# Order of the input norm's squares, one weight load and a small cast behind the splits of x, in a hybrid decoder block

## The chip, the cores and the metric

One core of a Trainium2 chip runs the whole block. The metric is the device time of one launch in microseconds (us): 1686.27 us, the median of 3 runs of the kernel before (1686.22 to 1686.97).

## The reference, cut to what matters

The block takes x (1024 tokens by 1024 channels, float32), forms u = rms_norm(x) and multiplies it with a wide weight matrix w_in, whose columns feed attention, a gated convolution and merge gates:

```python
def rms_norm(x, g):
    y = x * rsqrt(mean(x * x, axis=-1) + EPS)
    return y * g

u = rms_norm(h, norm_mix_g)
z = u @ w_in
q, kc, vc, ks, vs, kw, vw, nsa_g, glu_in, merge_g = split(z, offsets)
y_a = nsa_attention(...) @ w_a
y_b = conformer_conv(glu_in, ...) @ w_b
h = h + (sigmoid(g_a) * y_a + sigmoid(g_b) * y_b) @ w_o
```

After that come a convolutional feed-forward part, a gated per-layer input and a last norm. The change lies in the first 40 us, at the first rms_norm and the first two products of z.

## The kernel before, in words

**Layout.** Channels lie on the 128 partitions and tokens in the free dimension. x is loaded transposed, as KD = 8 tiles of 128 channels by 1024 tokens (tile names H for the first four, M for the last four).

**Split numbers.** A float32 product is made from two reduced-precision parts. `split_gain` (L190) makes from a tile of x, times the norm's gain, a high part uh on ScalarE (L193) and a low part ul on VectorE (L194); all of them carry the tile names U. `load_w` (L123) loads 128 columns of a weight matrix with a DMA of the SP queue (L125), and `split_w` makes wh on ScalarE (L119) and wl on GpSimd (L120). `product` (L133) then issues for each of the 8 tiles of x six matmuls of 512 tokens: wh with uh (L139) and wh with ul (L140) for each half of the tokens, and wl with uh for both halves (L142). So a product has 48 matmuls.

**The norm's factor comes late.** The splits use x and the gain alone. The factor Rs = 1/sqrt(mean x^2 + EPS) is multiplied in when a product leaves PSUM. For it, `add_sq` (L207) squares each half of a tile on ScalarE (L198 for the first tile, L201 for the others) and adds it to one of two running sums, sq[0] on VectorE and sq[1] on GpSimd (both L202). The temporary squares have the tag PW, of which there are four buffers, two of them held by the sums. `rstd_part` (L163) then does for each half of the tokens: eight small matmul instructions with ones (L170), a VectorE step (L172), a power on GpSimd (L173), eight small matmul instructions that spread the factor over the partitions (L176), and a copy into Rs on ScalarE (L178).

**Order at the start.** L212 to L234 load the first weights, then the eight tiles of x with their splits (the first two tiles half by half); after the sixth tile the second weights are loaded. The squares of tile k are queued behind the split of tile k + 2 with `queued_after` (L183), which fixes the order on an engine's queue and waits for nothing. The order on all engine queues is fixed when the program is built, by a list scheduler that follows a modelled timeline and prefers earlier lines among the instructions that are ready; every engine then works its own queue strictly in that order.

**What follows.** A loop over j (L360 to L375) makes two products for each of four column groups of the gated convolution; below they are called pa0, pb0, pa1, pb1, pa2 and so on. They share two PSUM buffers (psA). For j = 0 ScalarE copies the product out of PSUM at once (L355) and VectorE multiplies it by Rs later (L356); for the others VectorE multiplies by Rs straight out of PSUM (L358), so such a product's buffer is free only after Rs is known. VectorE's next long work, the 31-tap convolution (L330, L333), is queued behind that. The positions are loaded by two small DMAs (L262, L263), cast to float on VectorE (L266) and turned into sines and cosines (L270 to L288).

Of the kernel before, what the change touches and what calls it, by code (L numbers as in the profile page):

```python
# [17 lines left out]
P = 128  # L18
T = 1024
D = 1024  # L20
KD = D // P
# [11 lines left out]
C_Q, C_KC, C_VC, C_SEL, C_WIN, C_GLU, C_GA, C_GB = 0, 512, 640, 768, 1024, 1304, 2328, 3352  # L33
# [22 lines left out]
def block_kernel(ctx, tc, xT, pT, pos, par_d, w_in, ck1, ck2, cv1, cv2, w_a, w_b, w_o, w_up, w_down,  # L56
                 w_pg, w_pp, outT):
    nc = tc.nc
# [21 lines left out]
    def t(tag, shape, dt=F32):  # L80
        count[0] += 1
        return where.get(tag, sb).tile(shape, dt, name=f"{tag}_{count[0]}", tag=tag, bufs=BUFS.get(tag, 1))
# [33 lines left out]
    def split_w(raw, shape, hi_tag="wh", lo_tag="wl", eng=nc.gpsimd):  # L116
        hi = t(hi_tag, shape, F32R)
        lo = t(lo_tag, shape, F32R)
        nc.scalar.activation(hi, raw, AF.Copy)  # L119
        eng.tensor_tensor(lo, raw, f(hi), op=OP.subtract)  # L120
        return hi, lo

    def load_w(src, shape, hi_tag="wh", lo_tag="wl", raw_tag="raw", eng=nc.gpsimd):  # L123
        raw = t(raw_tag, shape)
        nc.sync.dma_start(raw, src)  # L125
        return split_w(raw, shape, hi_tag, lo_tag, eng)
# [17 lines left out]
    def wcols(w, c0, n, k0=0, k1=KD):  # L144
        return w[k0 * P:k1 * P, c0:c0 + n].rearrange("(k p) c -> p k c", p=P)
# [37 lines left out]
    def queued_after(*marks):  # L183

        st = ExitStack()
        for m in marks:
            st.enter_context(tc.issue_after(m.ins))
        return st

    def split_gain(j, src, goff, uh, ul):  # L190

        g = par[:, goff + j:goff + j + 1]
        hi = nc.scalar.activation(uh, src, AF.Copy, scale=g)  # L193
        return hi, nc.vector.scalar_tensor_tensor(ul, src, g, f(uh), op0=OP.mult, op1=OP.subtract)  # L194
# [12 lines left out]
    def add_sq(j, src, sq, *engs):  # L207
        for hf in range(2):
            add_sq_half(j, src, sq, hf, engs[hf % len(engs)])
# [7 lines left out]
    xts, split_marks = [], []  # L217
    w_first = load_w(wcols(w_in, C_GLU, P), [P, KD, P])
    for k in range(KD):
        xt = t("H" if k < 4 else "M", [P, T])  # L220
        for s in HALF if k < 2 else [slice(0, T)]:
            nc.sync.dma_start(xt[:, s], xT[k * P:(k + 1) * P, s])
            marks = split_gain(k, xt[:, s], O_GMIX, uh[k][:, s], ul[k][:, s])
        xts.append(xt)
        split_marks.append(marks)
        if k == 5:
            w_second = load_w(wcols(w_in, C_GLU + 512, P), [P, KD, P])
    for k in range(KD):
        with queued_after(*split_marks[min(k + 2, KD - 1)]):
            add_sq(k, xts[k], sq, nc.vector, nc.gpsimd)  # L230
    norm_marks = [m for m in rstd(sq) if m.ins.engine != nc.vector.engine]
    nc.vector.tensor_scalar(rTs, rT, 0.125, None, op0=OP.mult)
# [27 lines left out]
    posi = sb.tile([P, NP], I32, name="posi")  # L260
# [2 lines left out]
    nc.sync.dma_start(posi[0:N_CMP, NCH:NP],  # L263
                      bass.AP(tensor=pos.tensor, offset=pos.offset + 31, ap=[[16, N_CMP], [1, 1]]))
    posf = sb.tile([P, NP], F32, name="posf")
    nc.vector.tensor_copy(posf, posi)  # L266
    tg = t("PW", [P, 256])
    inv = tg[:, 0:8]
    for i in range(8):
# [642 lines left out]
    with tc.manual_schedule(engines={nc.tensor.engine, nc.scalar.engine, nc.vector.engine, nc.gpsimd.engine}):  # L912
# [8 lines left out]
        for i in range(-1, len(jobs)):  # L921
# [6 lines left out]
            for s in range(n):  # L928
                rest = None
                k = s - (n - len(outs))  # L930
# [666 lines left out]
```

## Time and profile before

| what | value |
|---|---|
| median of 3 runs | 1686.27 us |
| the profiled execution's own time | 1692.59 us |
| its span in the profile | 1690.9 us |
| TensorE busy in it | 1636.3 us, 97% |
| VectorE, ScalarE, GpSimd busy | 1189.1, 712.7, 668.7 us |
| mean granted TensorE clock | 0.989 of full speed |

The span is what the hardware profiler saw of one execution; the execution itself took 1.7 us more, and it is 6.3 us above the median of the runs without a profile. PE is TensorE, DVE VectorE, ACT ScalarE, POOL GpSimd and SP the engine that issues the DMAs. A busy engine is one with an instruction in progress, so a PE that is busy at half its clock still counts as busy: the granted clock has to be read beside it.

### The profile page before, as it was taken

To read this page: it belongs to the slowest core of one execution; us is meant where nothing else is said; L and a number is where in the kernel's file an instruction comes from. 1 tells how busy PE (TensorE), PEld (TensorE's weight loads), DVE (VectorE), ACT (ScalarE), POOL (GpSimd) and SP (SyncE) were. 2 spreads that over 40 slices of the span, in tenths; PEclk is the share of its full clock that TensorE was granted. 3 is DMA by queue.
4 is the path that set the end of the run, shared out by engine and by line. 5 is a ranking of instruction groups with operands and counts; after the bars stand their busy time and mean duration, and the time that the engine had idled before them with its cause. 6 is when DMAs were issued, how large, how long until landed. Compare 5 with 4: busy or idle time off the path is not lost.

```text
span 1690.9 us, 23161 instructions
## 1 busy us (share of the span) xinstructions
PE 1636.3 (97%) x8506; PEld 1377.1 (81%) x8506; DVE 1189.1 (70%) x1885; ACT 712.7 (42%) x1202; POOL 668.7 (40%) x602
## 2 busy tenths in 40 slices
PE   7999989999999999999999999999999999999997
PEld 5888989888888788877877888888888778888887
DVE  6799895355677777653368766766667878887756
ACT  6222343555566655523345333343334322223522
POOL 5524345344443343346441232222322344445600
PEclk9999999999999999999999999999999999999998
DMA  6122212322111221146443333333333844443113
GB/s 204 51 63 65 76 54 63 116 82 61 45 52 54 72 76 51 45 162 199 132 154 115 112 100 121 116 100 112 100 115 127 319 149 143 142 141 117 45 38 125
DMA packets 172378, 178.03 MB, mean 105 GB/s; under 512 B 24936, under 2 KB 138728, under 8 KB 172264
## 3 DMA queue, kind: packets, MB, share of 16 engines
q1 hardware_dynamic: 171400, 173.40, 32.0%
q10 hardware_dynamic: 864, 3.15, 0.5%
q8 instruction: 67, 1.10, 0.3%
q14 instruction: 47, 0.39, 0.1%
HBM read 128.29 MB, written 48.23 MB: 104 GB/s over the span
## 4 chain that ended last, share of the span: by engine, by line
PE 82%; DVE 5%; issue 4%; POOL 3%; ACT 3%; DMA 3%; SPq 0%; POOLq 0%; DVEq 0%; ACTq 0%
PE psB L1123 8%; PE psB L1125 8%; PE psB L1124 8%; PE psF L694 7%; PE psO L1428 4%; PE psO L1427 4%; PE psO L1430 4%; PE psA L142 4%; PE psA L140 4%; PE psA L139 4%; PE psO L888 3%; PE psS L791 3%; PE psPT L877 3%; PE psF L728 3%; PE psA L131 3%
## 5 line engine op out<-in xcount | busy, mean ns | idle before, releaser
L1011 POOL TENSOR_TENSOR A<-r,A 128x512 fp32r<-128x512 f32 x65 | 114.4, 1760 | 315.2 <-ACT A L1007 315.2
L120 POOL TENSOR_TENSOR wl<-raw,wh 128x1024 fp32r<-128x1024 f32 (+1 forms) x58 | 143.9, 2483 | 142.3 <-ACT wh L119 142.2
L333 DVE SCALAR_TENSOR_TENSOR conv<-PS,par,conv 128x1023 f32<-128x1023 f32 (+14 forms) x120 | 152.6, 1272 | 3.5
L882 DVE TENSOR_TENSOR PT<-psPT,PT 128x512 fp32r<-128x512 f32 (+1 forms) x136 | 91.6, 674 | 76.6 <-ACT PT L879 75.4
L1007 ACT ACTIVATE S<-psX 128x512 fp32r<-128x512 f32 x88 | 52.6, 598 | 211.7 <-DVE psX L1056 139.0
L119 ACT ACTIVATE wh<-raw 128x1024 fp32r<-128x1024 f32 (+1 forms) x58 | 61.3, 1058 | 148.3 <-PE psA L140 66.5
L694 PE MATMUL psF<-U,wh 128*128 128x512 f32 x352 | 118.9, 400 | 0.0
L879 ACT ACTIVATE PT<-psPT 128x512 fp32r<-128x512 f32 (+1 forms) x136 | 79.3, 584 | 91.3 <-PE psPT L877 86.0
L1161 DVE SCALAR_TENSOR_TENSOR M<-H,par,M 128x1023 f32<-128x1023 f32 x88 | 115.0, 1308 | 0.1
L1123 PE MATMUL psB<-T,S 128*128 128x512 f32 x264 | 104.3, 395 | 5.0 <-DVE H L1166 5.0
L791 PE MATMUL psS<-K,Q 128*128 128x384 f32 (+3 forms) x384 | 105.7, 356 | 0.0
L1125 PE MATMUL psB<-T,S 128*128 128x512 f32 x264 | 104.2, 395 | 0.0
L1124 PE MATMUL psB<-T,S 128*128 128x512 f32 x264 | 103.5, 392 | 0.0
L1428 PE MATMUL psO<-fs,X 128*128 128x512 f32 x256 | 100.5, 392 | 2.4 <-DVE fs L1264 2.4
L1427 PE MATMUL psO<-fs,X 128*128 128x512 f32 x256 | 100.4, 392 | 0.0
L139 PE MATMUL psA<-U,wh 128*128 128x512 f32 x224 | 90.1, 403 | 8.2 <-ACT U L193 7.9
L1011 DVE TENSOR_TENSOR S<-psX,S 128x512 fp32r<-128x512 f32 x88 | 60.7, 690 | 50.3 <-ACT S L1007 50.3
L888 PE MATMUL psO<-PT,V 128*128 128x256 f32 x528 | 91.7, 291 | 2.7 <-DVE PT L882 2.6
L812 POOL TENSOR_SCALAR PS<-PS,rr,gates 128x128 f32<-128x128 f32 (+7 forms) x64 | 52.2, 825 | 103.0 <-DVE rr L808 59.9
L140 PE MATMUL psA<-U,wh 128*128 128x512 f32 x224 | 89.8, 402 | 3.0 <-DVE U L194 3.0
L1166 DVE TENSOR_TENSOR H<-PW,psB 128x512 f32<-128x512 f32 x66 | 45.3, 687 | 55.2 <-PE psB L1125 55.0
L1260 POOL TENSOR_TENSOR F<-F,F 128x1024 f32<-128x1024 f32 x18 | 43.3, 2405 | 100.7 <-issue 74.3
(464 smaller groups left out, 4905.6 us busy)
## 6 DMA issues: line engine op xcount, KB each, us to landing
r<-in_w_up SPq DMA_DIRECT2D x44, 512.0 KB, 4.8
raw<-in_w_in SPq DMA_DIRECT2D x32, 512.0 KB, 3.6
g_d<-M SPq DMA_DIRECT2D x22, 512.0 KB, 2.6
a_d<-M SPq DMA_DIRECT2D x22, 512.0 KB, 3.0
raw<-in_w_o SPq DMA_DIRECT2D x16, 512.0 KB, 4.0
F<-g_d SPq DMA_DIRECT2D x16, 512.0 KB, 4.2
F<-a_d SPq DMA_DIRECT2D x16, 512.0 KB, 3.4
raw<-in_w_down SPq DMA_DIRECT2D x16, 512.0 KB, 4.2
```

The source lines that it names most:

```text
L120: eng.tensor_tensor(lo, raw, f(hi), op=OP.subtract)
L139: nc.tensor.matmul(pz[:, s], hi, xh[k][:, s], start=k == 0, stop=False)
L140: nc.tensor.matmul(pz[:, s], hi, xl[k][:, s], start=False, stop=False)
L333: nc.vector.scalar_tensor_tensor(a[:, s:], y[:, :T - s], w, a[:, s:], op0=OP.mult, op1=OP.add)
L694: nc.tensor.matmul(pz, wa[:, k, :], ua[k][:, s], start=k == 0 and i == 0, stop=k == KD - 1 and i == 2)
L791: nc.tensor.matmul(pS[:, :n * P], Q[:, h, v, :], K[:, i0 * P:(i0 + n) * P], start=v == 0, stop=v == 1)
L1011: return eng.tensor_tensor(o[:, 1, :], src, f(o[:, 0, :]), op=OP.subtract)
L1123: nc.tensor.matmul(pz, hi, xh, start=first and k == 0, stop=False, skip_group_check=True)
L1124: nc.tensor.matmul(pz, hi, xl, start=False, stop=False, skip_group_check=True)
L1125: nc.tensor.matmul(pz, lo, xh, start=False, stop=last and k == 3, skip_group_check=True)
L1427: nc.tensor.matmul(pd, ws[i][0][:, js], fs[i][0][:, s], start=i == 0, stop=False)
L1428: nc.tensor.matmul(pd, ws[i][0][:, js], fs[i][1][:, s], start=False, stop=False)
```

## The change

All eight splits of x come first on ScalarE and VectorE. The second weights' load is moved from behind the sixth tile of x to behind the eighth, and what it puts on ScalarE is queued behind the last split there. All the norm's squares and VectorE's part of their sums are queued behind the last split, instead of behind the split two tiles on. The positions' cast on VectorE is queued behind the last split too.

```diff
             marks = split_gain(k, xt[:, s], O_GMIX, uh[k][:, s], ul[k][:, s])
         xts.append(xt)
         split_marks.append(marks)
-        if k == 5:
-            w_second = load_w(wcols(w_in, C_GLU + 512, P), [P, KD, P])
+    x_split = split_marks[-1]
+    with queued_after(*x_split):
+        w_second = load_w(wcols(w_in, C_GLU + 512, P), [P, KD, P])
     for k in range(KD):
-        with queued_after(*split_marks[min(k + 2, KD - 1)]):
+        with queued_after(*x_split):
             add_sq(k, xts[k], sq, nc.vector, nc.gpsimd)
...
     posf = sb.tile([P, NP], F32, name="posf")
-    nc.vector.tensor_copy(posf, posi)
+    with queued_after(*x_split):
+        nc.vector.tensor_copy(posf, posi)
```

`x_split` holds the last ScalarE and the last VectorE instruction of the splits, so GpSimd's and SP's queues get no such edge: GpSimd's share follows through the data that it needs, and the DMAs follow the order of the lines.

## Rows read from the trace of the kernel before

**Rows 1.** The profile's first part: busy us, share of the span, instructions, by engine.

```profile
PE 1636.3 (97%) x8506; PEld 1377.1 (81%) x8506; DVE 1189.1 (70%) x1885; ACT 712.7 (42%) x1202; POOL 668.7 (40%) x602
```

**Rows 2.** Waits, 0 to 60 us: total us, times, longest.

```profile
PE psA L140 <- DVE U L194: 3.0, 3, 1.8
```

**Rows 3.** Stretches: length, busy by engine (instructions), granted clock, DMA share, GB/s.

```profile
24.33:29.01 4.68, 4.68 (x14) 3.71 (x14) 3.98 (x4) 1.86 (x4) 2.76 (x2) 0.64 0.52 132
...
30.00:100.00 70.00, 70.00 (x320) 57.35 (x319) 53.20 (x57) 21.16 (x25) 36.06 (x20) 1.00 0.23 64
```

**Rows 4.** Timeline of TensorE: start, length (us), operation, [idle before <- releaser].

```profile
14.58 0.40 PE L139 MATMUL psA<-U,wh 128*128 128x512 f32 x1
...
24.33 0.50 PE L140 MATMUL psA<-U,wh 128*128 128x512 f32 x1 [1.83 <-DVE U L194]
...
38.34 0.95 PE L170 MATMUL psF<-ones,PW 128*128 128x1 f32 x8
...
39.70 0.40 PE L139 MATMUL psA<-U,wh 128*128 128x512 f32 x1
...
43.83 0.72 PE L170 MATMUL psF<-ones,PW 128*128 128x1 f32 x6
...
51.44 1.05 PE L176 MATMUL psPT<-ident,rT 128*128 128x128 f32 x8
...
53.50 0.39 PE L139 MATMUL psA<-U,wh 128*128 128x512 f32 x1
...
64.71 0.40 PE L139 MATMUL psA<-U,wh 128*128 128x512 f32 x1
```

**Rows 5.** Timeline of VectorE, 18 to 62 us: splits, the cast, a sum, an evacuation.

```profile
18.40 1.28 DVE L194 SCALAR_TENSOR_TENSOR U<-M,par,U 128x1024 fp32r<-128x1024 f32 x1
19.60 1.26 DVE L266 CAST posf<-posi 128x9 f32<-128x9 int32 x1
20.91 3.37 DVE L194 SCALAR_TENSOR_TENSOR U<-M,par,U 128x1024 fp32r<-128x1024 f32 x1
...
32.19 1.34 DVE L202 TENSOR_TENSOR PW<-PW,PW 128x512 f32<-128x512 f32 x1 [0.70 <-ACT PW L201]
...
61.20 1.23 DVE L358 TENSOR_TENSOR Q<-psA,Rs 128x1024 f32<-128x1024 f32 x1
```

**Rows 6.** Timeline of GpSimd, 18 to 39 us: sums and a low part of weights.

```profile
18.97 1.86 POOL L202 TENSOR_TENSOR PW<-PW,PW 128x512 f32<-128x512 f32 x1 [2.86 <-ACT PW L201]
20.79 2.40 POOL L120 TENSOR_TENSOR wl<-raw,wh 128x1024 fp32r<-128x1024 f32 x1
...
36.91 1.28 POOL L202 TENSOR_TENSOR PW<-PW,PW 128x512 f32<-128x512 f32 x1
```

**Rows 7.** Timeline of ScalarE, 21 to 54 us.

```profile
21.83 1.13 ACT L193 ACTIVATE U<-M,par 128x1024 fp32r<-128x1024 f32 x1
...
28.93 1.18 ACT L201 ACTIVATE PW<-M 128x512 f32<-128x512 f32 x2 [0.51 <-POOL PW L202]
30.97 1.18 ACT L201 ACTIVATE PW<-M 128x512 f32<-128x512 f32 x2 [0.85 <-POOL PW L202]
33.41 1.06 ACT L119 ACTIVATE wh<-raw 128x1024 fp32r<-128x1024 f32 x1 [1.25 <-PE psA L140]
...
39.81 0.26 ACT L288 ACTIVATE cosT<-PW 128x72 f32<-128x72 f32 x1 [1.00 <-DVE PW L287]
...
52.53 0.60 ACT L178 ACTIVATE Rs<-psPT 128x512 f32<-128x512 f32 x1 [6.34 <-PE psPT L176]
```

**Rows 8.** Timeline of SP's queue: DMA issues of the second weights and the last two x tiles.

```profile
7.07 0.38 SPq L125 DMA_DIRECT2D raw<-in_w_in  x1
7.78 3.41 SPq L222 DMA_DIRECT2D M<-in_xT  x2
```

**Rows 9.** DMA issues (6.9 to 7.4, 7.4 to 10.7 us): count, size, us to landing.

```profile
raw<-in_w_in SPq DMA_DIRECT2D x1, 512.0 KB, 9.0
...
M<-in_xT SPq DMA_DIRECT2D x1, 512.0 KB, 9.6
```

## The prediction

> **What bounds the kernel now.** I read the shares of busy time first: TensorE is busy for 97% of the span and no other engine for more than 70% [rows 1], so time can be won mainly where TensorE waits or runs at half clock. The table by stretches comes next: from 30 to 100 us TensorE is busy without a gap at full clock [rows 3]. Whatever it is ahead by at 35 us it can therefore keep, as long as nothing else is late in that stretch. Last I read the timelines of the four engines up to 65 us, which hold the changed lines. The reader should see a collision there. TensorE has its longest wait of the start, 1.83 us, until 24.33 us, for the low split of the seventh tile of x [rows 2, 4]. That split took 3.37 us on VectorE where the one before took 1.28 us, and in front of it the nine-element cast of the positions took 1.26 us [rows 5]. Beside the cast GpSimd was adding squares until 20.83 us, and the cast ends at 20.86 us; beside the slow split GpSimd was making the second weights' low part until 23.19 us, and the split ends 1.09 us later [rows 5, 6]. After that wait TensorE ran for 4.68 us at a mean granted clock of 0.64, so partly at the lower of its two levels, 1.2 and 2.4 GHz; before the drop it had been waiting [rows 3, 4].
>
> By the Trainium skill, page "SBUF — State Buffer", section "Who interferes with whom", a VectorE instruction with two SBUF inputs and a GpSimd instruction that reads SBUF exclude each other for a whole instruction. The two pairs of rows just named agree with it. If the slow split had another cause that stays, the eighth low part would come 2.1 us later than reckoned below, 0.3 us after TensorE wants it, and the sum would be 0.3 us smaller.
>
> **What the splits gain.** Products pa0 and pb0 have 96 matmuls. I count 12 issued before the one at 14.58 us, so 84 lie between it and the first of pa1 at 39.70 us: 25.12 us [rows 4]. At full clock a product of 48 takes 64.71 - 53.50 = 11.21 us, or 0.2335 us a matmul [rows 4]. 84 of them are 19.62 us; with 0.95 us for the eight small matmuls of the norm that stand among them [rows 4] it is 20.57 us. **So 4.55 us are there to be won.** About 1.7 us of it is the half clock (4.68 x 0.36), 2.3 us are waits, the rest is the restart after each.
>
> Is the data there in time? DMA: the second weights were issued at 7.07 us and landed 9.0 us later, at 16.1; the seventh tile was issued at 7.78 and landed at 17.4 [rows 8, 9]. All are 512 KB, so in the new order the seventh tile takes the place at 16.1 us, the eighth that at 17.4, the weights follow 1.3 us later at 18.7. SP's queue issues as many DMAs as before, and the positions' two stay behind them. Splits: with nothing in between, the eighth tile's high part is done at 17.4 + 1.13 = 18.5 us [rows 7] and the low part at 19.8 (1.28 us, no GpSimd beside it [rows 5]). TensorE, from 14.58 us on without a gap, comes to the eighth tile after 30 matmuls, at 21.6 us. Cover 1.8 us: cost nothing, and if a landing slips by more than that, every further microsecond shows. Second weights: the high part takes 1.06 us [rows 7], from 18.7 us or behind the first tile's two squares, so 19.8 to 20.9; the low part takes 2.40 us [rows 6], so 22.2 to 23.3. TensorE wants the high part at 23.0 and the low part four matmuls later, at 23.9. I take nothing; the ends are 0 and 1 us. The cast runs for a moment behind the last split; the sines that use it are not wanted by these products: nothing, either end below 0.3 us.
>
> **What the squares cost.** Sixteen squares, seven VectorE sums and seven GpSimd sums move behind 18.5 us. With four PW buffers the pace is the alternation that the rows show near the end: 2.04 us from one pair of squares to the next (28.93 to 30.97) [rows 7]. The first GpSimd sum waits for the second weights' low part, so it ends at 23.5 to 24.6 us; six more pairs take 12.2 us: 35.7 to 36.8 us, and 2.40 us more if pa1's low part is put between them as now, so 38.1 to 39.2. Before it was 36.91 + 1.28 = 38.2 us [rows 6]. VectorE's sum, last done at 33.5 us before [rows 5], comes about 1 us ahead of GpSimd's, so 34.7 to 38.2 us. TensorE's first small matmuls (L170) stood at 38.34, those of the second half at 43.83 [rows 4]; 4.55 us earlier that is 33.8 and 39.3. If the first keep their place in TensorE's queue, they wait 0.9 to 4.4 us, and every product matmul waits behind them; if the scheduler moves them back with the squares, nothing. TensorE never waited for them before, and stood 4.8 us behind the sum. The same modelled order sees the squares later, so I take 0.5 us, near the lower end; the ends are 0 and 4.4.
>
> **What is late next.** Rs's second half was made at 52.53 us, behind small matmuls that stood at 51.44 us in TensorE's order [rows 4, 7]. VectorE then empties pa1 until 61.20 + 1.23 = 62.43 us [rows 5], and pa2, which needs that buffer, starts at 64.71 [rows 4]. The cover is 2.28 us; beyond it Rs has to come earlier by as much as TensorE does. As its matmuls stand in TensorE's own order they move along, so I charge nothing; without that, the gain is cut to 2.28 us.
>
> **Sum.** 4.55 - 0.5 = 4.05 us. The profiled execution took 1692.59 us and would take 1688.5; the median lies 6.3 us lower, so I forecast 1686.27 - 4.05 = **1682.2 us**. Later parts follow TensorE, but the scheduler may order them a little differently; I bound that by one low part of weights, 2.4 us, either way [rows 6].
>
> **Rivals.** A: Rs stays at its hour. For it: VectorE and GpSimd's new chain of sums ends no earlier than before. Against: the sums were done at 38.2 us, and Rs came 14 us later [rows 6, 7], so there is room. Gain 2.28 us: 1684.0.
>
> B: TensorE's order keeps the first norm matmuls in place while the sums come late. For it: GpSimd's two low parts of weights now fall among the deferred sums, and the slow split of 3.37 us [rows 5] shows what VectorE pays beside one. Then VectorE's last sum is at 38.2 us, TensorE waits 4.4 of the 4.55 us: 1686.1 us, and with a drop of the clock as after 24.33 us (1.7 us) 1687.8. Against: the order was made for the new lines.
> The exclusion that the Trainium skill states on "SBUF — State Buffer" speaks for this rival: by it the deferred sums of the two engines, and the low parts among them, cannot overlap. No row before shows eight pairs of sums in a run, so here the rule goes further than the trace.
>
> C, slower: pa1's weights end up behind all squares and the sines. Their high part was made at 33.41 us, in a gap of the squares [rows 7]; behind the cosine, which came 6.3 us after VectorE's last sum (39.81 against 33.5 [rows 5, 7]), it would begin at about 35 + 6.5 = 41.5 us, and the low part end at 41.5 + 1.06 + 2.40 = 45.0. TensorE wants it at 35.15 + 0.93 = 36.1: 8.9 us late, and 1.7 us of half clock: 4.55 - 10.6, so 1692.3 us. It is slower than before once the low part ends after 39.0 us (36.1 + 4.55 - 1.7). Against: the buffer for these weights is free once pa0 is done, at 23 us, and ScalarE has gaps between squares (0.51 and 0.85 us [rows 7]).
>
> **How the numbers follow.** Forecast 0.52, A 0.15, B 0.22, C 0.11. The forecast's own range is 1680.7 to 1683.5. Over all, the lower end is the full 4.55 us and 2.4 us more from later order, 1679.3; the upper end is B with 2.4 us, 1688.5; C lies mostly outside. A measurement of this kernel tells about 0.2%, 3.4 us, from no change: faster means under 1682.9, slower over 1689.6. Of the forecast's chance 0.47 lies under that line and 0.01 of A's; C gives 0.09 of slower; the rest, 0.43, is the same.
>
> **What would show it.** Right: in the new timeline the L194 splits all take about 1.28 us, the eighth is done by 20 us, TensorE has no wait between 15 and 35 us, the granted clock stays at 1.00 from 20 to 30 us, pa1 starts at about 35, Rs's second half comes before 50.8. Wrong: a wait of TensorE at L170 (B), at the first L139 of pa2 for VectorE's L358 (A), at the first L139 or L142 of pa1 for ScalarE or GpSimd (C); or a start of pa1 at 35 us with the gain gone by 300 us, which I have no step for.

## The result, and the profile after

| | median us | range (runs) | ratio to before, 95% interval |
|---|---|---|---|
| before, beside it | 1686.49 | 1686.22 to 1686.97 (4) | |
| after | 1698.38 | 1694.42 to 1700.88 (4) | 1.0062 [1.0049, 1.0076] |
| after, on a second chip | 1697.60 | 1695.41 to 1698.96 (4) | 1.0058 [1.0042, 1.0074] |

The change makes the kernel about 10 to 12 us slower. The forecast was 1682.2 us and the range ended at 1688.5: both the sign and the range were wrong. One run in each of two experiments was disturbed (1814.6 and 2303.5 us) and is left out, among them the profiled one of the squares alone, so that experiment has a time but no profile to compare with the others.

The profiled execution after took 1694.42 us (span 1692.7), at a mean granted clock of 0.989. Line numbers after are one or two higher than before from L225 on. The first part of the page, which answers to [rows 1], does not show that anything happened:

```profile
PE 1634.9 (97%) x8506; PEld 1376.3 (81%) x8506; DVE 1189.8 (70%) x1885; ACT 712.7 (42%) x1202; POOL 668.4 (39%) x602
```

The timeline of VectorE after, from the last splits to the start of the long convolution (start, length in us, operation, idle before and its releaser), answers to [rows 5]:

```profile
14.32 4.86 DVE L194 SCALAR_TENSOR_TENSOR U<-M,par,U 128x1024 fp32r<-128x1024 f32 x4
19.11 0.16 DVE L268 CAST posf<-posi 128x9 f32<-128x9 int32 x1
...
38.19 2.19 DVE L277 TENSOR_TENSOR PW<-posf,PW 128x72 f32<-128x72 f32 x1
...
44.05 0.15 DVE L172 TENSOR_SCALAR rT<-psF 128x4 f32<-128x4 f32 x1
...
55.75 4.57 DVE L358 TENSOR_TENSOR Q<-Q,Rs 128x1024 f32<-128x1024 f32 x2 [5.92 <-ACT Rs L178]
...
63.74 2.35 DVE L360 TENSOR_TENSOR Q<-psA,Rs 128x1024 f32<-128x1024 f32 x2
66.01 1.34 DVE L332 TENSOR_SCALAR conv<-PS,par 128x1024 f32<-128x1024 f32 x1
```

The first two rows are the intended effect, and it is complete. Four splits in a row take 4.86 us, one every 1.2 us, the eighth is done at 14.32 + 4.86 = 19.18 us, and the cast takes 0.16 us where it took 1.26. The rest is the price: the product pa1 is emptied from 63.74 us on where it was 61.20 [rows 5].

The timeline of TensorE after, its rows that answer to [rows 4] (the view of the second row ends before the last of its eight matmuls):

```profile
24.80 0.51 PE L139 MATMUL psA<-U,wh 128*128 128x512 f32 x1 [1.22 <-ACT Q L357]
...
40.87 0.83 PE L170 MATMUL psF<-ones,PW 128*128 128x1 f32 x7
...
46.42 0.72 PE L170 MATMUL psF<-ones,PW 128*128 128x1 f32 x6
...
54.03 1.05 PE L176 MATMUL psPT<-ident,rT 128*128 128x128 f32 x8
...
65.11 0.77 PE L139 MATMUL psA<-U,wh 128*128 128x512 f32 x1 [3.96 <-DVE Q L360]
```

The wait of 1.83 us for the seventh split is gone. A new one of 1.22 us stands at 24.80: the scheduler now puts the first four matmuls of pa1 among those of pb0, and they need the PSUM buffer that pa0 is still being copied out of. Then come the norm's small matmuls, all 2.5 to 2.6 us later on the clock than before (40.87 against 38.34, 46.42 against 43.83, 54.03 against 51.44), although TensorE itself is ahead. At the first matmul of pa2 TensorE waits 3.96 us for VectorE to empty pa1.

The table by stretches (length, busy time and instructions of PE, PEld, DVE, ACT and POOL, granted clock, DMA share, GB/s), after:

```profile
24.33:29.01 4.68, 4.21 (x18) 3.45 (x19) 3.01 (x2) 2.51 (x5) 3.32 (x3) 1.00 0.86 222
...
64.70:100.00 35.30, 34.89 (x139) 28.10 (x140) 32.79 (x26) 4.24 (x4) 14.98 (x8) 0.91 0.17 45
```

The half clock at 24 to 29 us of [rows 3] is gone, but from 64.7 us on, at the end of the new wait at pa2 and behind it, the granted clock is 0.91 over 35 us, in which TensorE has 139 matmuls.

A second loss lies 150 us further on. The waits of TensorE from 200 to 300 us (total us, times, longest), before:

```profile
PE psPT L575 <- ACT PW L572: 7.5, 3, 3.8
```

and after:

```profile
PE psPT L577 <- ACT PW L574: 9.1, 3, 4.1
```

The timeline of ScalarE shows where it comes from. Before:

```profile
218.54 1.03 ACT L335 ACTIVATE H<-conv 128x1024 f32<-128x1024 f32 x1
...
222.54 1.34 ACT L572 ACTIVATE PW<-M 128x256 f32<-128x256 f32 x4 [1.18 <-POOL M L313]
```

and after, with the row of Rs that answers to [rows 7] ahead of it:

```profile
55.12 0.60 ACT L178 ACTIVATE Rs<-psPT 128x512 f32<-128x512 f32 x1 [5.39 <-PE psPT L176]
...
226.59 1.02 ACT L337 ACTIVATE H<-conv 128x1024 f32<-128x1024 f32 x1 [1.86 <-DVE conv L335]
227.51 1.32 ACT L574 ACTIVATE PW<-M 128x256 f32<-128x256 f32 x4
```

VectorE begins its convolution at 66.01 us instead of 62.34 and hands over its third filter's result only at 226.6 us instead of 218.5. Only part of these 8 us is the later start: on the way VectorE itself waits for late products, once for 2.15 us at 90.5 us (L360). ScalarE's copy of that result (L337) waits for it, and in ScalarE's queue the four key copies (L574) stand directly behind that copy. Those are what TensorE waits for. Before, the copy waited for nothing, another copy (L557) stood between it and the keys, and the keys waited for GpSimd. This chain is read from the rows; no run moves the copy by itself.

**Against which execution?** The profile of before that the prediction used took 1692.59 us. A second profiled execution of the same kernel took 1686.06 us, close to its median. Its table by stretches has this row in the place of the first of [rows 3]:

```profile
24.33:29.01 4.68, 4.68 (x22) 3.78 (x21) 3.82 (x4) 2.46 (x5) 2.16 (x2) 1.00 0.50 146
```

and its timeline of TensorE, the last small matmuls and the first matmul of pa2:

```profile
49.24 1.05 PE L176 MATMUL psPT<-ident,rT 128*128 128x128 f32 x8
...
62.51 0.40 PE L139 MATMUL psA<-U,wh 128*128 128x512 f32 x1
```

The seventh split is as slow there (3.37 us, a wait of 1.85 us), but no half clock follows: 22 matmuls in the 4.68 us instead of 14. So pa2 starts at 62.51 us and not at 64.71, and VectorE's convolution at 60.15. This is the execution to compare with; it is called the typical one below. Without its wait TensorE after would have started pa2 at 65.11 - 3.96 = 61.15 us: the start really wins 62.51 - 61.15 = 1.4 us (0.6 us in the second profiled execution of after, e5 below, where pa2 starts at 65.92 behind a wait of 3.97). With the wait it is 2.6 us behind. The last row of VectorE's L504 (L506 after) stands at 174.0 us in the typical execution and at 179.6 after, 5.6 us later, and between pa2 and there TensorE waits for nothing in either. So 5.6 - 2.6 = 3.0 us go with the clock, as 0.09 of the 35.3 us at 0.91 (3.2 us) also says. ScalarE's last L604 (L606 after) stands at 300.5 and 308.7, 8.2 us later; the end comes 8.4 us later. **So the loss is made by 300 us: 5.6 us at pa2 and behind it, 2.6 us around the keys.** Of these 2.6 us the longer wait for the keys is 1.6 (9.1 against 7.5); the clock from 200 to 300 us is 0.97 against 0.98.

### The profile page after: what moved, and what is told of

Read it like the earlier page. It is cut to its first block, busy times and chain, and to the rows that moved or that the text cites. A ratio compares the mean times of both kernels' runs of the same rounds, so it can differ in the third digit from the quotient of the medians.

```text
span 1692.7 us, 23165 instructions
## 1 busy us (share of the span) xinstructions
PE 1634.9 (97%) x8506; PEld 1376.3 (81%) x8506; DVE 1189.8 (70%) x1885; ACT 712.7 (42%) x1202; POOL 668.4 (39%) x602
## 4 chain that ended last, share of the span: by engine, by line
PE 84%; DVE 5%; issue 4%; ACT 2%; POOL 2%; DMA 2%; POOLq 0%; DVEq 0%; SPq 0%; ACTq 0%
PE psB L1125 8%; PE psB L1127 8%; PE psB L1126 8%; PE psF L696 7%; PE psO L1430 4%; PE psO L1429 4%; PE psO L1432 4%; PE psA L140 4%; PE psA L139 4%; PE psA L142 4%; PE psO L890 3%; PE psS L793 3%; PE psPT L879 3%; PE psF L730 3%; PE psA L130 3%
## 5 line engine op out<-in xcount | busy, mean ns | idle before, releaser
L890 PEld LDWEIGHTS psO<-PT,V 128*128 128x128 f32 x528 | 76.6, 189 | 7.4 <-DVE PT L884 4.9
```

What stands on the lines that cost most here:

```text
L890: nc.tensor.matmul(pO[:, cols], vst[br, kb // 4][:, kb % 4, g, :], pt[:, a, x], start=False, stop=last and x == m - 1 and a == 1, skip_gro ...
```

## The experiments

**The parts alone.** Each of these three undoes two of the three parts of the change, so that one is left.

The squares alone (label e1_squares), against after:

```diff
+        if k == 5:
+            w_second = load_w(wcols(w_in, C_GLU + 512, P), [P, KD, P])
     x_split = split_marks[-1]
-    with queued_after(*x_split):
-        w_second = load_w(wcols(w_in, C_GLU + 512, P), [P, KD, P])
...
-    with queued_after(*x_split):
-        nc.vector.tensor_copy(posf, posi)
+    nc.vector.tensor_copy(posf, posi)
```

> Only the squares and their sums are queued behind the last split; the second weights and the cast stay as in the kernel before. In TensorE's queue the last of the norm's spreading matmuls (L176) stands after 178 product matmuls here, after 139 in the kernel before and after 166 in the changed one. Theory 1 (the norm's factor Rs comes later, so pa2 waits for VectorE to empty pa1): this part alone is enough for the loss; Rs's second half comes at 56 to 61 us against 52.5 before, TensorE waits 4 to 8 us at the first matmul of pa2, and the time is 1693 to 1700. Theory 2 (the move of the second weights costs): 1685 to 1688, no wait at pa2. Theory 3 (the order of later stages changed, the start is not to blame): any time, but no wait over 1 us at pa2.

The second weights alone (e2_weights): the squares keep `queued_after(*split_marks[min(k + 2, KD - 1)])` and the cast has no edge.

> Only the second weights' load is moved behind the last split of x; squares and cast stay as in the kernel before. The last spreading matmuls stand after 152 product matmuls (139 before, 166 in the changed kernel). Theory 1: in between; TensorE is ahead by some 2 us at 35 us and Rs comes within 1 us of before, so pa2 waits 0 to 2 us: 1685 to 1690. Theory 2: the whole loss, 1694 to 1700. Theory 3: any time, with no wait over 1 us at pa2.

The cast alone (e3_cast): squares and second weights as before.

> Only the positions' cast is queued behind the last split; TensorE's queue has the norm's matmuls where the kernel before has them (after 139 product matmuls). All theories: the seventh split is still slow beside GpSimd's second low part, since that stays. Theory 1: 1685 to 1687, the cast's 1.26 us may be won in part. Theory 3 would allow a change of some us in either direction though nothing at the start differs.

| label | median us (runs) | before beside it | ratio, 95% interval |
|---|---|---|---|
| e1_squares | 1694.58 (6) | 1688.27 (28) | 1.0037 [1.0025, 1.0048] |
| e2_weights | 1689.57 (10) | 1688.27 | 1.0005 [0.9993, 1.0017] |
| e3_cast | 1688.16 (10) | 1688.27 | 0.9997 [0.9986, 1.0008] |

The deferred squares carry most of the loss, 6.3 us. The weights and the cast alone change nothing that can be told (the 1685 to 1687 us expected of the cast was missed, but before itself stood at 1688.27 on this chip). Neither of the two frees the splits by itself: the timeline of VectorE of the cast alone still has

```profile
20.11 3.36 DVE L194 SCALAR_TENSOR_TENSOR U<-M,par,U 128x1024 fp32r<-128x1024 f32 x1 [1.23 <-ACT U L193]
```

and that of the weights alone

```profile
21.95 3.47 DVE L194 SCALAR_TENSOR_TENSOR U<-M,par,U 128x1024 fp32r<-128x1024 f32 x1
```

each beside a GpSimd instruction. The three parts add up to 7.5 us against 10 to 12 for the whole, though the squares alone put the last spread still further back in TensorE's queue than the whole change does (table below); how the rest is split between an interplay of the parts and the scatter between chips stays open.

**Is it the place in TensorE's queue?** The order of the built programs gives the place of the norm's small matmuls by the number of product matmuls ahead of them:

| kernel | first half (L170) | second half (L170) | last spread (L176) |
|---|---|---|---|
| before | 94 | 114 | 139 |
| the cast alone | 94 | 114 | 139 |
| the weights alone | 107 | 127 | 152 |
| the squares alone | 133 | 153 | 178 |
| after | 121 | 141 | 166 |
| after with two edges (e4, e6 below) | 121 | 126 | 144 |

In after they are 27 product matmuls further back, 27 x 0.2335 = 6.3 us; less the 1.4 us of head start that is 4.9 us, and the last spread came 54.03 - 49.24 = 4.8 us later than in the typical execution. The next kernel (e4_norm_early) leaves the change as it is and adds two edges on TensorE's queue: pa1's matmuls from the sixth tile of x on come behind the last L170, and pb1 behind the last L176.

```diff
-            for s in HALF:
+            with queued_after(*behind.get(k, ())):
+                for s in HALF:
...
-        pa = z_tile(*wa)
+        pa = z_tile(*wa, behind={5: (norm_f,)} if j == 1 else {})
...
-        pb = z_tile(*wb)
+        pb = z_tile(*wb, behind={0: (norm_pt,)} if j == 1 else {})
```

> The changed kernel with one thing added: pa1's matmuls from the sixth tile on are queued behind the norm's small matmuls of the second half (L170), and pb1's behind its spreading matmuls (L176), so that these stand after 144 product matmuls instead of 166. The sums are ready at 41.5 us, so they should not be waited for. Theory 1: Rs's second half comes 5 to 6 us earlier than in the changed kernel, at 49 to 50.5 us, the wait of 4.0 us at pa2 and the half clock behind it (3 us) are gone: 1681 to 1688, at least 7 us under the changed kernel. Theories 2 and 3: within 3 us of the changed kernel's 1698.4.

Measured: 1690.84 us (10 runs), ratio to before 1.0015 [1.0003, 1.0027]. That is some 7 us better than after but outside the 1681 to 1688 us expected, and Rs came at 54.28 us and not at 49 to 50.5. The timeline of TensorE says why (the lines are three higher here, L173 is L170 and L179 is L176):

```profile
44.19 1.84 PE L173 MATMUL psF<-ones,PW 128*128 128x1 f32 x8 [1.49 <-DVE rT L175]
...
53.19 1.05 PE L179 MATMUL psPT<-ident,rT 128*128 128x128 f32 x8
```

with the timeline of VectorE:

```profile
43.78 0.20 DVE L293 TENSOR_SCALAR PW<-PW 128x72 f32<-128x72 f32 x1
43.89 0.15 DVE L175 TENSOR_SCALAR rT<-psF 128x4 f32<-128x4 f32 x1
```

The second half's matmuls need the PSUM tile of the first, which VectorE reads in a step of 0.15 us, and that step stands in VectorE's queue behind the steps of the sines (L293 is the last of them). TensorE waits 1.49 us with all its products behind, and its clock is 0.75 from 40 to 53.4 us. At pa2 it waits only 0.30 us, since it comes there late itself.

**With VectorE's queue mended too.** e6_early_trig adds one more edge, which puts the sine steps behind the norm's VectorE steps; e7_trig has this edge without the two of TensorE; e5_after_again is the changed kernel itself on the same chip.

```diff
+    rstd_marks = rstd(sq)
...
+    trig_queue = queued_after(*[m for m in rstd_marks if m.ins.engine == nc.vector.engine])
+    trig_queue.__enter__()
     tg = t("PW", [P, 256])
...
     nc.scalar.activation(cosT, ang, AF.Sin)
+    trig_queue.__exit__(None, None, None)
```

> The changed kernel once more, unaltered, beside the kernels of this group on one chip. Theory 1 (Rs is late because the norm's matmuls stand further back in TensorE's queue) and the others: as in its first measurement, 8 to 13 us over the kernel before; a wait of about 4 us at the first matmul of pa2 for VectorE's L360, and half clock behind it.

> The changed kernel with the norm's matmuls drawn forward as in e4, and the sine and cosine steps on VectorE queued behind the norm's two VectorE steps (L172), which in e4 stood behind them and came at 43.9 us for sums ready at 40.5. Theory 1: the norm's second set of matmuls no longer waits 1.5 us, the half clock of 40 to 53 us is gone, Rs's second half comes at 48 to 50 us and pa2 does not wait; the 4 to 5 us won at the start stay: 1681 to 1686, under the kernel before. A rival to it (the head start is lost later anyway, by VectorE's convolution or the order of later stages): at or over the kernel before, 1687 to 1692, though the start is clean.

> The changed kernel with only the sine and cosine steps queued behind the norm's VectorE steps; TensorE's queue is the same, with the last spreading matmuls after 166 product matmuls. Theory 1 says the place in TensorE's queue decides, not how soon the sums or the factor are ready: Rs's second half within 1 us of the changed kernel's 55.1, pa2 waits 3 to 4.5 us, time as the changed kernel within 2 us. Rival (VectorE's late factor step at 44.05 us holds Rs): Rs 2 us or more earlier, time 3 us or more under the changed kernel.

The last of this set, e8_copy, leaves Rs as late as it is and frees the PSUM buffer instead: ScalarE copies pa1 out at once, as it does pa0, and VectorE multiplies by Rs later.

```diff
-        ya = t("Q", [P, T])
-        times_r(ya, pa, j == 0)
+        ya = t("PS" if j == 1 else "Q", [P, T])
+        times_r(ya, pa, j <= 1)
```

> The changed kernel in which ScalarE copies pa1 out of PSUM into a buffer of its own, as it does with pa0 and pb0, and VectorE multiplies it by Rs later; so pa2's buffer is free when ScalarE has copied it. ScalarE does that behind the first tanh (at 60.4 us in the changed kernel), so at about 62.4 us against 65.0. Theory 1 (it is this buffer that TensorE waits for): the wait at pa2 falls from 4.0 to 1 to 2 us, and the time by 2 to 4 us under the changed kernel. If another thing holds pa2 (its weights' low part), the wait stays at 3 us or more.

| label | median us (runs) | ratio to before (1687.45, 19 runs) | last spread, us | wait at pa2, us | TensorE's waits for the key copies, us |
|---|---|---|---|---|---|
| e5_after_again | 1697.60 (4) | 1.0058 [1.0042, 1.0074] | 54.83 | 3.97 | 9.1 |
| e6_early_trig | 1687.36 (10) | 0.9993 [0.9978, 1.0007] | 48.78 | 0.28 | 7.5 |
| e7_trig | 1695.29 (4) | 1.0049 [1.0033, 1.0065] | 54.04 | 3.96 | 9.1 |
| e8_copy | 1691.92 (10) | 1.0025 [1.0011, 1.0039] | 54.83 | 1.23 | 10.4 |

With all three edges the whole loss is gone, 10.2 us against after on the same chip. The time itself is not in the 1681 to 1686 us that were expected but in the rival's range (1687 to 1692), though not because a head start was lost later: the 4 to 5 us that both counted as won were never there (e12 below). The timeline of TensorE of e6_early_trig:

```profile
42.80 0.95 PE L173 MATMUL psF<-ones,PW 128*128 128x1 f32 x8
...
48.78 1.05 PE L179 MATMUL psPT<-ident,rT 128*128 128x128 f32 x8
...
61.31 0.48 PE L140 MATMUL psA<-U,wh 128*128 128x512 f32 x1 [0.28 <-DVE Q L368]
```

and of VectorE, the first step of the sines that reads the positions:

```profile
44.10 0.24 DVE L284 TENSOR_TENSOR PW<-posf,PW 128x72 f32<-128x72 f32 x1
```

22 places in the queue are 5.1 us, and the last spread came 54.03 - 48.78 = 5.25 us earlier than in after (6.05 us against the 54.83 of e5, where TensorE ran 0.8 us later by then). The clock stays at 1.00 from 40 to 100 us. e7_trig is the control: with the sine steps out of the way but the matmuls at places 121, 141 and 166, the last spread and the wait at pa2 stay where they were. Its median is 2.3 us under that of e5, a little more than the 2 us expected, but the two intervals overlap. So Rs was late by its place in the queue, not because its inputs were late; the sine steps only come to matter once the place is mended.

e8_copy separates the two losses. The buffer is free earlier, pa2 starts at 63.18 us and the clock stays at 1.00 from 64.7 to 100 us; 5.7 us of the 10 come back, more than the 2 to 4 expected. But VectorE still gets Rs at 55.92 us, and has a 3.43 us multiplication instead of one of 1.2, so the convolution begins later still, at 68.84 us (66.83 in e5_after_again). The waits of TensorE from 200 to 300 us:

```profile
PE psPT L577 <- ACT PW L574: 10.4, 3, 5.4
```

and ScalarE's timeline there:

```profile
223.14 1.02 ACT L337 ACTIVATE H<-conv 128x1024 f32<-128x1024 f32 x1 [3.16 <-DVE conv L335]
224.06 1.33 ACT L574 ACTIVATE PW<-M 128x256 f32<-128x256 f32 x4
```

By VectorE's last L506, which waits for a product of TensorE, TensorE is 4.3 us ahead of e5 (174.9 against 179.2), the third filter's result only 3.0 us, and the wait for the keys is 1.3 us longer. So the second loss stands here without the first. A late start of the convolution is not enough for it: in e4 the convolution starts at 65.50 us, and the waits for the keys are as before:

```profile
PE psPT L581 <- ACT PW L578: 7.5, 3, 3.8
```

Nor is it needed: in e9 below it starts at 60.47 us, the copy still waits 3.40 us, and the waits for the keys are 8.2 us. By these rows it depends on when that result comes and on what the scheduler has queued behind its copy.

**Is there a version that beats before?** e9_all_three adds to e6 an edge that puts pa1 behind the last matmul of pb0, against the wait at 24.80 us. e10_early_trig_again repeats e6 on a third chip. e11_before_early gives the kernel before such edges, with its squares, weights and cast where they were; there the last spread stands at place 132 instead of 139.

```diff
-        pa = z_tile(*wa, behind={5: (norm_f,)} if j == 1 else {})
+        pa = z_tile(*wa, behind={0: (pb0_last,), 5: (norm_f,)} if j == 1 else {})
```

> The changed kernel with three more edges: the norm's matmuls drawn forward and the sines queued behind the norm's VectorE steps, as in e6, and pa1's matmuls queued behind the last of pb0, because in e6 TensorE still waited 1.22 us at 24.7 us for ScalarE to empty pa0 (the scheduler had put pa1's first four matmuls between those of pb0). Theory 1: no wait over 0.5 us between 15 and 65 us except at pa2, where VectorE may be up to 1.5 us late; ahead of the kernel before by 5 to 6.5 us at 300 us, 1681 to 1685. Rival (a head start under 5 us is lost again later, in VectorE's convolution or by the clock behind later waits): no faster than the kernel before within 2 us.

> The kernel of e6 once more with more rounds, since its interval (0.9978 to 1.0007) holds both a gain of 3.5 us and nothing, while its trace was 4 us ahead of the kernel before at 300 us. Theory 1: 2 to 5 us under the kernel before. Rival (the head start is lost later): within 1.5 us of it.

> The kernel before, none of the change in it, with the same edges as in e9: sines behind the norm's VectorE steps, norm's spreading matmuls after 132 product matmuls instead of 139, pa1 behind pb0. TensorE does not wait at pa2 in the kernel before, so theory 1 expects no more than VectorE's convolution starting 1 to 2 us sooner: within 2 us of the kernel before. If an early Rs were worth something by itself, without the splits in front, it would be 3 us or more faster.

| label | median us (runs) | ratio to before (1687.82, 29 runs) |
|---|---|---|
| e9_all_three | 1686.95 (11) | 0.9996 [0.9984, 1.0008] |
| e10_early_trig_again | 1685.82 (10) | 0.9990 [0.9978, 1.0002] |
| e11_before_early | 1686.85 (12) | 0.9997 [0.9986, 1.0008] |

All three lie about 1 to 2 us under before, and every interval holds no change. e9 misses the 1681 to 1685 us expected, and the gain of 2 to 5 us expected of e10 is not shown (2.0 us, in an interval that holds none). In e9 the wait for pa0's copy is gone, but TensorE waits 1.55 us for GpSimd's low part of weights instead. None is shown to be faster.

**A second profile of before** (e12_before_again) has no edit. It is the execution used in the section above.

> The kernel before, unaltered, for a second profile of it: its one profile so far is of an execution of 1692.6 us, 4 to 5 us over its usual time, and it is not known in which stretch. If its surplus lies after 300 us, the new trace stands within 1 us of the old one at 64.7 and at 299 us, and the leads that the traces of e6 and e9 show at 300 us (3 to 5 us) are real and lost later. If it lies before, the new trace is 2 to 4 us earlier at 299 us, and those leads are 1 to 2 us.

It took 1686.06 us and stands 2.2 us ahead of the first profile at pa2 and 3.1 us at ScalarE's last L604 (300.5 against 303.6), so about half of the first one's surplus of 6.5 us lay before 300 us. In its first 30 us the granted clock was 1.00, in those of the first profile 0.94. By VectorE's last L504 and ScalarE's last L604 (their lines there are ten higher), e6 and e10 are 1.1 to 1.7 us ahead of it. That is about what was won at the start; their medians, 0.1 and 2.0 us under before, neither show it nor speak against it.

## Why the prediction was wrong

**The splits: right.** Those of whole tiles took 1.27 us each, the eighth was done at 19.18 us for the 19.8 reckoned, the wait for the seventh was gone and the clock was 1.00 from 24 to 29 us. The Trainium skill, page "SBUF — State Buffer", section "Who interferes with whom", was drawn on for this, and the trace agrees a second time, in a place that the prediction did not look at. By the page, a VectorE instruction with two SBUF inputs and a GpSimd one that reads SBUF shut each other out. The 72-element product of the sines took 2.19 us beside GpSimd's low part of weights (37.60 to 40.29 us) and 0.24 us in e6, where that stood elsewhere. Two things do not fit so well. In e6 the product ran beside a GpSimd power of 128x4, which reads SBUF too (44.03 to 45.04 us), and was not held. And of the two pairs of rows with which the prediction backed the rule, the cast has only one SBUF input, so the rule as given there does not speak of it.

**"So 4.55 us are there to be won": mis-sized, 0.6 to 1.4.** The prediction measured this in one execution, 6.3 us slower than its median, and took the gain from the median. The half clock (1.7 us of it) is not in the typical execution, where the same 84 matmuls and the eight small ones lose about 2.5 us (23.09 from 14.43 us on, for 20.57). Of that the new wait at 24.80 takes 1.22 us back, a wait in front of pa1 that no step had: the step assumed that pa1 would start after pb0.

**The squares' 0.5 us: right in its sign, and empty.** TensorE never waited at L170, so rival B did not come. VectorE's sums ended at 38.0 us (34.7 to 38.2 reckoned), GpSimd's at 41.5, 2.3 us behind the end of the range, because three low parts of weights ran before the last sum where the end of the range had two (a pair from 21.04 to 25.78 us, and the one below), and two steps from sum to sum took 2.65 us instead of 2.04:

```profile
33.54 1.29 POOL L202 TENSOR_TENSOR PW<-PW,PW 128x512 f32<-128x512 f32 x1 [1.36 <-ACT PW L201]
36.19 1.29 POOL L202 TENSOR_TENSOR PW<-PW,PW 128x512 f32<-128x512 f32 x1 [1.36 <-ACT PW L201]
37.60 2.69 POOL L120 TENSOR_TENSOR wl<-raw,wh 128x1024 fp32r<-128x1024 f32 x1
40.24 1.28 POOL L202 TENSOR_TENSOR PW<-PW,PW 128x512 f32<-128x512 f32 x1
```

The prediction said that "if the scheduler moves them back with the squares, nothing" is lost. It moved them back, and that is where the loss is.

**"What is late next": the step that failed.** It named the right place, the right cover (2.28 us at pa2) and the right wait, and then charged nothing, "as its matmuls stand in TensorE's own order they move along". Had they kept their places, they would have moved along. But the list was made anew with the squares deferred, and it put them 27 product matmuls later. TensorE's own lead and the lateness of Rs both use up the same cover: pa2 could start at 61.15 us instead of 64.71, 3.56 us earlier, and pa1 was emptied 2.5 us later or more (63.74 against 61.20), together 6.1 us against 2.28. The difference, 3.8 us, is the wait (3.96); in the typical execution the cover is the same 2.28 us (60.23 to 62.51). Rival A had this wait, but with Rs at its old hour; the hour moved too, so it stopped short of a loss.

**What came on top.** The clock behind that wait (3.0 us) had no term, though the prediction had seen a drop behind a wait and used it in rivals B and C. And the prediction read VectorE only up to the emptying of pa1. It noted that the cover ends there and not that the convolution, VectorE's main work from there to 227 us, would be late too. At the keys TensorE then waits 1.6 us longer in both profiles of after, and with the clock there the stretch costs 2.6 us in the one and 5.2 in the other (last L506 at 179.2, last L606 at 310.9, clock 0.93).

**Rival C** did not happen: TensorE waited for no weights at pa1. The slower side came by another mechanism than the one that was priced.

**What stays open.** The medians of after are 2 to 4 us above its profiled executions (1694.42 and 1695.41 us), with lower clocks in the runs without a profile (0.986 to 0.988 on the first chip), and where these fall can't be seen. Why the scheduler chose these places was not taken apart; that they decide the wait at pa2 was shown by moving them. The second loss, around the keys, goes when they are moved (e6), but its own chain was not tested by moving the copy.

## What to carry to other kernels

Where a scheduler fixes every queue, deferring a producer can also move its consumers to later places in other engines' queues, where they stay late even when their inputs are ready: fix the places of what hangs on a moved step, and check the next cover against the sum of both shifts, the head start and the lateness. Follow the late engine to the end of its long work, since a copy that waits for it holds up whatever stands behind it in its queue. And don't count as winnings what one execution lost: a half-clock stretch that a second profile does not have is not there to be won.

## What the hardware showed that was not expected

**One program, many times.** 76 runs of the kernel before on three chips took 1683.1 to 1692.6 us (mean 1688.2), and the time goes with the mean granted clock: runs at 0.993 average 1685.4 us, at 0.991 1688.0, at 0.989 1690.8. The three runs shown at first, within 0.8 us of each other, gave no hint of that; a measurement with four runs can be off by more than its own spread.

**The same wait, another clock.** After the same split of 3.37 us and nearly the same wait (1.83 and 1.85 us), the granted clock was 0.64 in one execution of before and 1.00 in the other, in the same stretch from 24.33 to 29.01 us. After the same 3.96 us at pa2 it was 0.91 from 64.7 to 100 us in one execution of after and 0.95 in the other; from 200 to 300 us the two had 0.97 and 0.93. So a wait in a trace prices its own length, and the clock behind it only as a range.
